# Seven block products in place of eight in both feed-forward layers of a two-block transformer chain, with the residual in DRAM meanwhile

## The chip, the cores and the metric

One core of a Trainium2 chip runs the whole chain in one launch. The metric is the device time of an execution in microseconds. Before the change the median of three runs is 2995.7 us (2993.17 to 2998.81). The engines are called as in the profile: PE multiplies matrices (PEld loads its weights beside it), DVE and ACT work on vectors, POOL is the general-purpose engine, SP issues transfers.

## The reference, cut to what matters

The first block (projections, an mLSTM branch, two attentions) is not touched. The second block has two layers; x is [1024 tokens, 1024 features], all float32:

```
h = modulate(rms_norm(x, norm1_g[0]), sh1, sc1);  x = x + g1 * s5_mixer(h)           # layer 0
h = modulate(rms_norm(x, norm2_g[0]), sh2, sc2);  x = x + g2 * swiglu(h)
h = modulate(rms_norm(x, norm1_g[1]), sh1, sc1);  x = x + g1 * short_conv_mixer(h)   # layer 1
h = modulate(rms_norm(x, norm2_g[1]), sh2, sc2);  x = x + g2 * swiglu(h)
return rms_norm(x, final_g)
def swiglu(h, w_in, w_out):      # w_in [1024, 2 * 2816], w_out [2816, 1024]
    g, u = jnp.split(h @ w_in, 2, axis=-1)
    return (jax.nn.silu(g) * u) @ w_out
```

The shifts, scales and gates of a layer come from one vector: mods = silu(c) @ w_ada[i] + b_ada[i].

## The kernel before, in words

**Operands.** Activations lie feature-major: a tile has 128 features on the partitions and 512 tokens (half of them) along a row; half 0 and half 1 are separate tiles. Every float32 operand of a product is an exact pair of parts, hi and lo: `Env.split` lets ACT copy the source to hi (L100) and DVE subtract to get lo (L108). `Env.mm3` (L110) then issues three matmuls, hi*hi, lo*hi, hi*lo (L114, L115, L116). So 128 x 128 weights against 512 tokens cost three matmuls, and `gemm` (L1629) runs eight such steps over the 1024 input features: 24 matmuls for 128 output features of 512 tokens.

**Feed-forward (`phase_ffn`, L1747).** The 2816 hidden features are 22 blocks f. `FGROUPS` (L31) puts them into groups of 5, 5, 4, 4, 4. For each f and each token half the kernel computes the gate (`pg`) and the value (`pu`), 48 matmuls, so 96 for one f; ACT takes silu of `pg` (L1765), DVE multiplies by `pu` (L1766), and the product is split into the pair `a`. The weights of one f come as two transfers of 512 KB and are split 128 x 1024 at a time. After a group the second product runs: 16 units `po` (eight output blocks, two token halves), each with three matmuls per f of the group, and DVE adds each result, times the gate, to the residual x, which stays in SBUF (L1788). In the last group the next norm is fed on the way: `Next.done` squares x on ACT and adds the squares on DVE (L220). In the second layer's last group token half 1 is cut in two parts of 256.

**Norms.** `Next.columns` sums the squares over the partitions on PE (`cs`, L159), DVE and POOL make 1/rms (L167, L170), DVE and PE spread it over the partitions (L193 to L200), and `Normed.pairs` (L1721) makes the pairs of the next product's input: a scalar_tensor_tensor on DVE (`hx`, L1739), a biased copy on ACT (L1742), a scalar_tensor_tensor on DVE (L1743). `Final` (L1839) is the last norm and the stores.

**The rest around it.** `phase_mixer` (L1639) ends with an output phase of 16 units of 48 matmuls. `phase_conv` (L1794) stands between the two feed-forward layers. `ada` (L1289) makes a layer's shifts and scales on DVE from 25 MB of weights, a step at each `e.tick()`; layer 1's run inside the first feed-forward layer, with tiles 512 wide. The pool of split weights, `e.wp`, lives on from phase to phase. Every engine works through its own queue in order; the order in the queues is set by a scheduler from the program order and not by hand here.

```
for f, h in seq:
    gemm(e, [ws[f][0]], hT, pg, h)
    gemm(e, [ws[f][1]], hT, pu, h)
    nc.scalar.activation(s, pg, AF.Silu)
    nc.vector.tensor_tensor(out=s, in0=pu, in1=s, op=ALU.mult)
    e.split(a[f][0][:, half(h)], a[f][1][:, half(h)], s)
```

Of the kernel before, what the change touches and what calls it, by code (L numbers as in the profile page):

```python
# [33 lines left out]
FGROUPS = [(0, 5), (5, 10), (10, 14), (14, 18), (18, 22)]  # L34


class Env:
    """Engines, pools, constants and DRAM operands shared by the phases."""
# [28 lines left out]

    def t2(self, name, dt=F32, w=HT):
# [16 lines left out]
    def psum(self, bufs):  # L85
        """A new set of PSUM pools: tag -> buffers."""
# [23 lines left out]
    def mm3(self, out, lhs, rhs, first, last):  # L110
        """out += lhs^T rhs, each operand an exact pair of parts."""
# [42 lines left out]
    def colsum(self, accs, name, tag="aux", n=4):  # L154
        """The sum of some [128, n * 128] -> PSUM columns [128 tokens, n] of sums over partitions."""
# [7 lines left out]
    def rstd(self, pc, pool, n, name, w=4):  # L163
        """(pc / n + eps) ** -0.5 of [128, w] columns."""
# [20 lines left out]
    def spread(self, r, pool, name, tag="aux", n=4):  # L185
        """The same by two products of exact parts, of n columns."""
# [51 lines left out]
# ---------------------------------------------------------------- block 1  # L238
def phase_projections(e):
    """Input norm, all input projections and the mLSTM branch."""  # L240
# [165 lines left out]
    def proj(m, name):  # L406
        """Feature-major projection block m: yields (half, PSUM)."""
# [20 lines left out]
    def proj_tok(evac):  # L428
        """Token-major projection to 256 columns; two token blocks a bank."""
# [17 lines left out]
    # z gates of the three branches, through DRAM, and the state-space tables  # L447
# [28 lines left out]
    # mLSTM: x_m, convolution, gates  # L476
# [20 lines left out]
    # mLSTM heads  # L497
# [13 lines left out]
    # on a row of both parts of a head's M: its negative, on every partition  # L511
# [8 lines left out]
    # gate weights folded through the q, k, v maps of each head  # L520
# [11 lines left out]
    for h in range(2):  # L532
        # the convolved and the plain inputs' parts side by side
# [45 lines left out]
    # decay of every (head, chunk) on all partitions  # L579
# [24 lines left out]
    def head(h4, prev):  # L604
# [9 lines left out]
        for h in range(2):  # L614
# [7 lines left out]
            # decay matrix, transposed: exp(a_s - M_t), s <= t  # L622
# [115 lines left out]
    # operands of the two attentions, through DRAM  # L738
# [18 lines left out]
def out_part(e, src, g, h, x, pair, done=None):  # L757
    """Adds branch g's part of the output projection to half h of x; yields between blocks."""
# [19 lines left out]
def phase_attention(e, r1, x, done):  # L778
    """Differential and memory attention, one half of the queries after the other; the output
    projection's parts that are ready fill the tensor engine. Gives y_d and y_c in DRAM."""  # L780
# [28 lines left out]
    # lambda on every partition  # L809
# [23 lines left out]
    class Diff:  # L833
        """One head and half of the differential attention; step j is queries j * 128 .. + 128."""
# [9 lines left out]
        def stages(self, j):  # L844
# [3 lines left out]
            def front():  # L848
                """Masked scores of both maps, their maxima and exponentials."""
# [5 lines left out]
                for c in range(nchunk):  # L855
# [3 lines left out]
                    for i, (a, b) in enumerate(((0, 0), (0, 1), (1, 0))):  # L859
                        # both maps side by side, each in its half of the rows  # L860
# [19 lines left out]
            def mid():  # L880
                """p0 - lam p1 l0 / l1, transposed."""
# [37 lines left out]
            def norm():  # L919
                """rmsnorm of od / l0, the gate."""  # L920
# [27 lines left out]
    class Mem:  # L948
        """One head and half of the memory attention; step i is queries i * 256 .. + 256."""
# [1103 lines left out]
```

## Time and profile before

| | |
|---|---|
| device time, median of 3 runs | 2995.7 us (2993.17 to 2998.81) |
| profiled execution: span (the page gives no other time of it) | 2994.1 us |
| PE busy | 2955.0 us, 14615 instructions |
| DVE busy | 1504.5 us, 2908 instructions |
| ACT busy | 950.5 us, 1692 instructions |
| POOL busy | 45.9 us, 62 instructions |
| mean DMA rate | 96 GB/s |
| mean granted PE clock | 0.990 of full speed |

The span runs from the first to the last instruction, and lies 1.6 us under the median of the runs. Busy times of PE add up records of pipelined matmuls that overlap, so the cost of a matmul is read from the distance of starts and not from the length of a record. The clock has two levels, 1.2 and 2.4 GHz; a figure between 0.5 and 1 is a mean over a stretch in which both were granted. The feed-forward layers begin at about 1172 and 2257 us; the convolution's products begin at 1904 us.

### The profile page before, as it was taken

The page shows a single profiled execution, that of the slowest core. Times are in us where ns is not written, and L with a number is a line of the kernel's source. Part 1 is how long each engine was busy: PE and PEld are TensorE (multiplying, and loading weights), DVE is VectorE, ACT ScalarE, POOL GpSimd, SP SyncE. Part 2 cuts the span into 40 slices and gives each one's busy share as a digit, 9 for nine tenths or more (in the row PEclk, how much of TensorE's full clock was granted, in tenths as well). Part 3 has the DMA queues.
Part 4 walks back from the last instruction along what each step waited for, and adds up shares of the span by engine and source line. Part 5 has one row for each costly group of instructions (what it writes and reads, how often), then busy time and mean ns, then how long its engine had stood idle before and what let it go on. Part 6 is the DMA issues. An engine that isn't in the chain of part 4 may idle for free.

```text
span 2994.1 us, 36875 instructions
## 1 busy us (share of the span) xinstructions
PE 2955.0 (99%) x14615; PEld 2419.5 (81%) x14615; DVE 1504.5 (50%) x2908; ACT 950.5 (32%) x1692; POOL 45.9 (2%) x62
## 2 busy tenths in 40 slices
PE   8999999999999999999999999999999999999999
PEld 7887788777777778888888888888888888888888
DVE  7988455588759845454443232722435232322324
ACT  6244652566646423211111112312323111111113
POOL 0000000000000000000000000000000000000000
PEclk9999999999999999999999999999999999999999
DMA  6465226643134621343331111111111111211111
GB/s 216 163 219 183 94 85 225 231 127 117 60 134 159 203 86 46 96 152 114 100 108 55 43 52 48 50 42 46 54 35 54 45 57 35 63 50 50 50 43 57
DMA packets 123334, 287.97 MB, mean 96 GB/s; under 512 B 12820, under 2 KB 30548, under 8 KB 122136
## 3 DMA queue, kind: packets, MB, share of 16 engines
q1 hardware_dynamic: 119576, 281.41, 29.5%
q10 hardware_dynamic: 3584, 4.20, 0.4%
q8 instruction: 115, 1.88, 0.3%
q14 instruction: 59, 0.48, 0.1%
HBM read 238.32 MB, written 47.24 MB: 95 GB/s over the span
## 4 chain that ended last, share of the span: by engine, by line
PE 83%; DVE 4%; issue 1%; DMA 1%; ACT 1%; POOL 0%; POOLq 0%; DVEq 0%; ACTq 0%; SPq 0%
PE po L114 5%; PE po L115 5%; PE po L116 5%; PE pu L115 5%; PE pu L114 5%; PE pu L116 5%; PE pg L114 5%; PE pg L115 5%; PE pg L116 5%; PE pout L114 1%; PE pout L115 1%; PE pout L116 1%; PE pS L863 1%; PE pgate L114 1%; PE pval L116 1%; PE pco L114 1%
## 5 line engine op out<-in xcount | busy, mean ns | idle before, releaser
L100 ACT ACTIVATE wh<-wraw 128x1024 fp32r<-128x1024 f32 (+2 forms) x285 | 270.0, 949 | 943.1 <-PE po L115 331.4
L108 DVE TENSOR_TENSOR wl<-wraw,wh 128x1024 fp32r<-128x1024 f32 (+2 forms) x285 | 308.4, 1083 | 293.4 <-ACT wh L100 290.8
L1766 DVE TENSOR_TENSOR silu<-pu,silu 128x512 f32<-128x512 f32 x88 | 60.8, 691 | 441.7 <-PE pu L116 441.7
L114 PE MATMUL po<-a,wh 128*128 128x512 f32 (+1 forms) x736 | 280.6, 381 | 0.0
L115 PE MATMUL po<-a,wh 128*128 128x512 f32 (+1 forms) x736 | 279.8, 380 | 0.0
L116 PE MATMUL po<-a,wl 128*128 128x512 f32 (+1 forms) x736 | 279.6, 380 | 0.0
L114 PE MATMUL pg<-f,wh 128*128 128x512 f32 x704 | 274.2, 389 | 0.0
L115 PE MATMUL pu<-f,wh 128*128 128x512 f32 x704 | 274.0, 389 | 0.0
L114 PE MATMUL pu<-f,wh 128*128 128x512 f32 x704 | 273.9, 389 | 0.0
L116 PE MATMUL pu<-f,wl 128*128 128x512 f32 x704 | 273.9, 389 | 0.0
L116 PE MATMUL pg<-f,wl 128*128 128x512 f32 x704 | 273.9, 389 | 0.0
L115 PE MATMUL pg<-f,wh 128*128 128x512 f32 x704 | 273.8, 389 | 0.0
L1788 DVE SCALAR_TENSOR_TENSOR x<-po,ada,x 128x512 f32<-128x512 f32 (+1 forms) x168 | 121.7, 725 | 203.3 <-PE po L116 203.2
L114 PEld LDWEIGHTS po<-a,wh 128*128 128x128 f32 x736 | 138.3, 188 | 30.1 <-ACT wh L100 3.2
L116 PEld LDWEIGHTS po<-a,wl 128*128 128x128 f32 x736 | 138.3, 188 | 26.3
L115 PEld LDWEIGHTS po<-a,wh 128*128 128x128 f32 x736 | 138.4, 188 | 26.0
L114 PEld LDWEIGHTS pg<-f,wh 128*128 128x128 f32 x704 | 132.0, 188 | 28.1 <-ACT wh L100 0.8
L114 PEld LDWEIGHTS pu<-f,wh 128*128 128x128 f32 x704 | 132.3, 188 | 27.5
L116 PEld LDWEIGHTS pg<-f,wl 128*128 128x128 f32 x704 | 132.3, 188 | 27.5
L115 PEld LDWEIGHTS pg<-f,wh 128*128 128x128 f32 x704 | 132.2, 188 | 27.4
L116 PEld LDWEIGHTS pu<-f,wl 128*128 128x128 f32 x704 | 132.0, 188 | 27.5
L115 PEld LDWEIGHTS pu<-f,wh 128*128 128x128 f32 x704 | 132.1, 188 | 27.3
(536 smaller groups left out, 5760.5 us busy)
## 6 DMA issues: line engine op xcount, KB each, us to landing
wraw<-in_w_ffn_in SPq DMA_DIRECT2D x88, 512.0 KB
wada<-in_w_ada SPq DMA_DIRECT2D x48, 512.0 KB
wada<-in_w_ada SPq DMA_DIRECT2D x96, 256.0 KB
wraw<-in_w_in SPq DMA_DIRECT2D x28, 512.0 KB
wraw<-in_w_out SPq DMA_DIRECT2D x48, 256.0 KB
wraw<-in_w_ffn_out SPq DMA_DIRECT2D x24, 512.0 KB
wraw<-in_conv_w_in SPq DMA_DIRECT2D x24, 512.0 KB
wraw<-in_w_ffn_out SPq DMA_DIRECT2D x32, 320.0 KB
```

The source lines that it names most:

```text
L100: i = self.nc.scalar.activation(*a, **k)
L108: nc.vector.tensor_tensor(out=lo, in0=src, in1=hi.bitcast(F32), op=ALU.subtract)
L114: nc.tensor.matmul(out, lh, rh, start=first, stop=False)
L115: nc.tensor.matmul(out, lh, rl, start=False, stop=False)
L116: nc.tensor.matmul(out, ll, rh, start=False, stop=last)
L863: nc.tensor.matmul(o[m], self.q[a][ms, qs], self.k[c][b][ms, 0:wc], start=(i == 0), stop=(i == 2 and not lastp))
L1766: nc.vector.tensor_tensor(out=s, in0=pu, in1=s, op=ALU.mult)
L1788: nc.vector.scalar_tensor_tensor(out=e.xt[m][:, tok], in0=pt, scalar=mod[:, 40 + m:41 + m], in1=e.xt[m][:, tok], op0=ALU.mult, op1=ALU.add)
```

## The change

Of one f the four results (gate and value, token half 0 and 1) are a 2 x 2 block matrix: rows gate and value, columns the token halves; the 1024 input features are the inner dimension, cut in two. The plain way takes eight products of half size, the new way seven (Strassen's method, in Winograd's form), each 12 matmuls: 84 for one f in place of 96.

- `Quad` replaces `Normed` before the feed-forward layers. It makes the norm's output in place in x's tiles, then forms the differences T1 to T4 of its blocks on DVE and splits seven kinds of block into pairs. Since x's tiles are used up by it, `Quad.done` first stores x to DRAM (`xd`) by 16 transfers of 256 KB from POOL's queue for each layer.
- `Weights` loads the weights of one f as four transfers of 256 KB, forms the sums S1 to S4 on DVE, and splits seven blocks of 128 x 512. Its pool is made anew for each feed-forward layer, and `e.wp` is released before it and made again for the convolution.
- `Unit` does the seven products of one f in the order 1 6 5 2 7 3 4 and combines them with seven additions on DVE, then as before silu, product and split.
- `ffn_head` does f = 0 in the plain way (96 matmuls) and f = 1 by seven products, interleaved, while `Quad`'s parts of the second token half are made.
- `FGROUPS` becomes 4, 4, 4, 4, 4, 2. In all groups but the last, ACT copies a unit of the second product out of PSUM times the gate (`ev`, three buffers), and a transfer from POOL's queue adds it to x in DRAM: 160 accumulating transfers of 256 KB in all. In the last group x is loaded back, and DVE adds to it as before.
- `ada` of layer 1 moves out of the feed-forward layer: its first half into the mixer's output phase, its second half into the convolution. The convolution copies four of x's blocks back into their first place (8 copies on ACT).

In the queues, PE has 10682 matmuls of 128 x 512 before and 10226 after, and 1538 of 128 x 256 before and 1442 after; DVE goes from 2814 instructions to 3483, SP from 815 to 985, POOL from 67 to 259.

```diff
-FGROUPS = [(0, 5), (5, 10), (10, 14), (14, 18), (18, 22)]
+FGROUPS = [(0, 4), (4, 8), (8, 12), (12, 16), (16, 20), (20, 22)]
...
+class Quad(Next):
...
+    def done(self, m, h):
+        super().done(m, h)
+        self.e.nc.gpsimd.dma_start(out=self.xd[m][:, half(h)], in_=self.x[m][h])
...
+    def make(self, h, r):
...
+        for k in range(4):
+            self.norm(h, k + 4, R)
+            self.parts2("11", k, x[k + 4][1])
+            if k % 2:
+                yield
+        for k in range(4):
+            self.norm(h, k, R)
+        for k in range(4):
+            tt(x[k + 4][1], x[k + 4][1], x[k][1], ALU.subtract)
+            tt(x[k][1], x[k][1], x[k][0], ALU.subtract)
+            self.parts2("T1", k, x[k][1])
+        yield
+        for k in range(4):
+            tt(x[k][0], x[k + 4][1], x[k][0], ALU.add)
+            self.parts2("T2", k, x[k][0])
+        for k in range(4):
+            self.parts2("T3", k, x[k + 4][1])
+        yield
+        for k in range(4):
+            tt(x[k + 4][0], x[k + 4][0], x[k][0], ALU.subtract)
+            self.parts2("T4", k, x[k + 4][0])
...
+            for o, a, b, op in (("S1", "10", "11", ALU.add), ("S2", "S1", "00", ALU.subtract),
+                                ("S3", "00", "10", ALU.subtract)):
+                nc.vector.tensor_tensor(out=st[o], in0=st[a], in1=st[b], op=op)
...
+class Unit:
+    order = "1652734"
+    left = dict(zip("1234567", ("00", "01", "S4", "11", "S1", "S2", "S3")))
+    right = dict(zip("1234567", ("00", "10", "11", "T4", "T1", "T2", "T3")))
...
+    def step(self, p):
...
+        product(e, b[p], self.W.take(), self.q, self.right[p], True, True)
...
+            e.nc.vector.tensor_tensor(out=t[o], in0=b["5" if o == "v" else p], in1=t[i], op=ALU.add)
...
-            gemm(e, [ws[f][0]], hT, pg, h)
-            inp.finish(NB)
-            gemm(e, [ws[f][1]], hT, pu, h)
...
+            ffn_head(e, W, inp, use(0), use(1))
+            fs = fs[2:]
+        for f in fs:
             e.tick()
+            Unit(e, W, q, use(f)).run(Unit.order)
...
+                t = e.ap.tile([P, HT], F32, tag="ev", name="ev", bufs=3)
+                nc.scalar.activation(t, pt, AF.Copy, scale=g)
+                nc.gpsimd.dma_start(out=inp.xd[m][:, tok], in_=t, accum_op=ALU.add)
...
+    u.run("65734")
```

**Order at the head of the first feed-forward layer, DVE.** The names: `f0v` is the variance behind the sums `cs` of token half 1, `f0R` the spread 1/rms, `f` the pairs of the norm's output, `raw` and `sum` weights as loaded and summed, `wl` their low parts, `ph` and `pu` results of products. Before, the rows behind that variance are:

```order
L167 TENSOR_SCALAR f0v<-cs 128x4
L1739 SCALAR_TENSOR_TENSOR hx<-x_5372,ada_4504,f0R 128x512
L1739 SCALAR_TENSOR_TENSOR hx<-x_5373,ada_4504,f0R 128x512
L1739 SCALAR_TENSOR_TENSOR hx<-x_5374,ada_4504,f0R 128x512
L1743 SCALAR_TENSOR_TENSOR f_11503<-hx,ada_4504,f_11502 128x512
```

After, some 60 rows behind the same variance (L172 there) stands a piece that has no counterpart before, with the sum S4 (L1868) and, three rows on, its low part:

```order
L2058 TENSOR_TENSOR p_11858<-ph_12059,p_11858 128x512
L2058 TENSOR_TENSOR p_11881<-ph_12086,p_11881 128x512
L113 TENSOR_TENSOR a_12056<-c_11999,a_12055 128x512
L1977 TENSOR_TENSOR p_11881<-p_11881,p_11858 128x512
L1868 TENSOR_TENSOR sum<-raw,sum 128x512
L1927 TENSOR_TENSOR uu<-pu_12115,p_11900 128x512
L113 TENSOR_TENSOR a_12056<-p_11881,a_12055 128x512
L113 TENSOR_TENSOR wl<-sum,wh 128x512
```

The last of these rows is the 76th instruction behind the variance, and product 3 of f = 1 on PE needs it.

**Order at the end of the first feed-forward layer, DVE and PE.** `po` are units of the second product, `c1sq` the sums of squares of token half 1, `cs` their sums over partitions, `pc`, `pv` and `pb` the convolution's first products. On DVE the last rows before the variance `cv` read, after the change:

```order
L2035 SCALAR_TENSOR_TENSOR x_16860<-po,ada_4504,x_16860 128x512
L225 TENSOR_TENSOR c1sq<-c1sq 128x512
L2035 SCALAR_TENSOR_TENSOR x_16861<-po,ada_4504,x_16861 128x512
L225 TENSOR_TENSOR c1sq<-c1sq 128x512
L2035 SCALAR_TENSOR_TENSOR x_16862<-po,ada_4504,x_16862 128x512
L225 TENSOR_TENSOR c1sq<-c1sq 128x512
L113 TENSOR_TENSOR wl<-wraw,wh 128x512
L172 TENSOR_SCALAR cv<-cs 128x4
```

They are as before but for the weight piece, 512 wide in place of 1024. PE's rows around that `cs` are, before:

```order
L114 MATMUL pb<-c_16126,wh 128x512
L115 MATMUL pb<-c_16127,wh 128x512
L159 MATMUL cs<-ones,c1sq 128x1 x8
L116 MATMUL pb<-c_16126,wl 128x512
L114 MATMUL pb<-c_16132,wh 128x512
```

and after:

```order
L119 MATMUL pv<-c_17007,wh 128x512
L120 MATMUL pv<-c_17008,wh 128x512
L119 MATMUL pb<-c_17007,wh 128x512
L120 MATMUL pb<-c_17008,wh 128x512
L164 MATMUL cs<-ones,c1sq 128x1 x8
L121 MATMUL pb<-c_17007,wl 128x512
L119 MATMUL pb<-c_17013,wh 128x512
```

Between the last `po` and the sums `cs` stood 24 of the convolution's matmuls, and now stand six.

## Rows read from the trace of the kernel before

**Rows 1.** The page's head: span; busy time, share and instructions of each engine.

```profile
span 2994.1 us, 36875 instructions
...
PE 2955.0 (99%) x14615; PEld 2419.5 (81%) x14615; DVE 1504.5 (50%) x2908; ACT 950.5 (32%) x1692; POOL 45.9 (2%) x62
```

**Rows 2.** PE's waits from 1000 us on: what for, total us, times, longest.

```profile
PE finR L199 <- DVE findh L193: 0.6, 1, 0.6
...
PE cs L159 <- ACT fin2sq L100: 0.2, 1, 0.2
```

**Rows 3.** Windows view: stretch, length, busy (count) by engine, PEclk, DMA share, GB/s.

```profile
990.00:1165.00 175.00, 175.00 (x773) 141.20 (x772) 93.41 (x119) 41.45 (x61) 1.01 (x1) 1.00 0.38 121
1290.00:1900.00 610.00, 609.42 (x2689) 499.51 (x2688) 235.38 (x311) 112.35 (x151) 1.01 (x1) 1.00 0.27 81
```

**Rows 4.** PE's timeline, end of the mixer: start, length (us); 31 starts apart.

```profile
1165.21 0.39 PE L115 MATMUL pgate<-yT,wh 128*128 128x512 f32 x1
...
1172.24 0.39 PE L116 MATMUL pval<-yT,wl 128*128 128x512 f32 x1
```

**Rows 5.** PE's timeline, last group of all: first unit, then 24 starts of 256.

```profile
2934.24 0.39 PE L114 MATMUL po<-a,wh 128*128 128x512 f32 x1
...
2936.96 0.28 PE L114 MATMUL po<-a,wh 128*128 128x256 f32 x1
...
2939.83 0.40 PE L114 MATMUL po<-a,wh 128*128 128x512 f32 x1
```

**Rows 6.** DVE's groups, 1290 to 1900 us: count, busy us, mean ns, idle.

```profile
L1788 DVE SCALAR_TENSOR_TENSOR x<-po,ada,x 128x512 f32<-128x512 f32 x76 | 56.9, 750 | 73.7 <-PE po L116 73.6
...
L1766 DVE TENSOR_TENSOR silu<-pu,silu 128x512 f32<-128x512 f32 x34 | 23.5, 691 | 162.0 <-PE pu L116 162.0
```

**Rows 7.** ACT's groups of the same stretch.

```profile
L100 ACT ACTIVATE a<-silu 128x512 fp32r<-128x512 f32 x34 | 21.5, 632 | 100.8 <-DVE silu L1766 100.8
```

**Rows 8.** DVE's timeline, start of the first feed-forward layer: start, length (us).

```profile
1172.73 0.75 DVE L1714 SCALAR_TENSOR_TENSOR sg<-pval,ada,sg 128x512 f32<-128x512 f32 x1 [3.42 <-PE pval L116]
1173.52 0.69 DVE L1716 TENSOR_TENSOR x<-x,sg 128x512 f32<-128x512 f32 x1
1174.13 1.22 DVE L108 TENSOR_TENSOR wl<-wraw,wh 128x1024 fp32r<-128x1024 f32 x1
1176.69 0.16 DVE L167 TENSOR_SCALAR f0v<-cs 128x4 f32<-128x4 f32 x1 [1.34 <-PE cs L159]
1176.77 2.06 DVE L1739 SCALAR_TENSOR_TENSOR hx<-x,ada,f0R 128x512 f32<-128x512 f32 x3
1178.74 2.07 DVE L1743 SCALAR_TENSOR_TENSOR f<-hx,ada,f 128x512 fp32r<-128x512 f32 x3
```

**Rows 9.** DVE's groups in the mixer's output phase, 1000 to 1172 us.

```profile
L1316 DVE SCALAR_TENSOR_TENSOR adacc<-wada,ada0c,adacc 128x1024 f32<-128x1024 f32 x20 | 25.7, 1284 | 14.4 <-DMA wada<-in_w_ada 14.3
```

**Rows 10.** Steps of the chain that ended last: start, length (us).

```profile
2960.84 1.53 PE cs L159 x14
...
2965.93 0.29 PE finR L200
...
2985.06 0.48 DVE x L1788
...
2988.27 0.75 DVE fin L1885
```

**Rows 11.** DVE's groups of 256 columns in the last 60 us.

```profile
L1788 DVE SCALAR_TENSOR_TENSOR x<-po,ada,x 128x256 f32<-128x256 f32 x16 | 7.7, 482 | 4.1 <-PE po L116 4.1
...
L220 DVE TENSOR_TENSOR fin2sq<-fin2sq 128x256 f32<-128x256 f32 x6 | 2.5, 423 | 1.4 <-ACT fin2sq L100 1.3
```

**Rows 12.** Windows view: a stretch of heavy transfers, two of many small products.

```profile
560.00:580.00 20.00, 20.00 (x103) 14.62 (x102) 17.09 (x47) 13.79 (x37) 0.00 (x0) 1.00 0.94 319
900.00:920.00 20.00, 18.81 (x149) 15.59 (x150) 18.35 (x20) 9.97 (x23) 1.31 (x6) 0.74 0.42 134
940.00:960.00 20.00, 18.32 (x191) 15.40 (x191) 19.86 (x26) 15.07 (x37) 3.30 (x6) 1.00 0.47 159
```

More of the change, by code (lines that the diff above doesn't have):

```diff
@@ L1366, in done @@
             self.finish()
-        self.sq[i].add(self.e.xt[m][:, self.parts[i]])
+        self.sq[i].add(self.e.xs(m, self.parts[i]))
         if m == NB - 1:
@@ new lines, in product, with __init__, run @@
+def product(e, out, w, q, c, first, last):
+    for k in range(4):
+        e.mm3(out, (w[0][:, k], w[1][:, k]), q[c, k], first and k == 0, last and k == 3)
+class Unit:
+    order = "1652734"
+    left = dict(zip("1234567", ("00", "01", "S4", "11", "S1", "S2", "S3")))
+    right = dict(zip("1234567", ("00", "10", "11", "T4", "T1", "T2", "T3")))
+    sums = {"6": [("u", "p")], "5": [("q", "u")], "2": [("p", "p")], "7": [("u", "u"), ("v", "u")],
+            "3": [("q", "q")], "4": [("u", "u")]}
+    done = {"2": "00", "7": "11", "3": "01", "4": "10"}
+    def __init__(self, e, W, q, use):
+        self.e, self.W, self.q, self.use, self.b, self.t = e, W, q, use, {}, {}
+    def run(self, ps):
+        for p in ps:
+            self.step(p)
+    def step(self, p):
+        e, t, b = self.e, self.t, self.b
+        b[p] = e.mm("mm", "pu" + p)
+        product(e, b[p], self.W.take(), self.q, self.right[p], True, True)
+        if p == "1":
+            t["p"] = e.t2("p1")
+            e.nc.scalar.activation(t["p"], b[p], AF.Copy)
+            return
+        for o, i in self.sums[p]:
+            if p == "2" and "u" not in t:
+                o = "c"
+            if o not in t:
+                t[o] = e.t2("u" + o)
+            e.nc.vector.tensor_tensor(out=t[o], in0=b["5" if o == "v" else p], in1=t[i], op=ALU.add)
+        if p in self.done:
+            self.use(self.done[p], t[o])
@@ L1744, in pairs, with phase_ffn, use, take @@
                                            op0=ALU.add, op1=ALU.subtract)
-def phase_ffn(e, L, mod, x, inp, nxt, mods=None):
-    nc, d, hT = e.nc, e.d, inp.hT
-    for gi, (f0, f1) in enumerate(FGROUPS):
-        a = {}
-        ws = {}
-        seq = [(f, h) for f in range(f0, f1) for h in range(2)]
+def phase_ffn(e, L, mod, inp, nxt, xp, last):
+    nc, d, q = e.nc, e.d, inp.q
+    W = Weights(e, 6, 6, 2, 3, 6)
+    e.ap = e.tc.alloc_tile_pool(name="ap", bufs=1, reuse_waits="tile")
+    src = lambda f: [d["w_ffn_in"][L, f + NF * i] for i in range(2)]
+    a = {}
+    def use(f):
+        s = {}
+        def take(n, t):
+            h = int(n[1])
+            s[h, int(n[0])] = t
+            if n[0] == "0":
+                nc.scalar.activation(t, t, AF.Silu)
+            if (h, 0) in s and (h, 1) in s:
+                nc.vector.tensor_tensor(out=s[h, 1], in0=s[h, 1], in1=s[h, 0], op=ALU.mult)
+                if f not in a:
+                    a[f] = tuple(xp.tile([P, T], F32R, tag="x", name=f"a{p}", bufs=NB) for p in range(2))
+                e.split(a[f][0][:, half(h)], a[f][1][:, half(h)], s[h, 1])
+        return take
+    std, u1 = W.unit(src(0), ("00", "10", "01", "11")), W.unit(src(1), [Unit.left[p] for p in "1265734"])
+    W.todo = [std[0], std[1], u1[0], std[2], std[3]] + u1[1:]
+    for gi, (f0, f1) in enumerate(FGROUPS):
+        for f in range(max(f0, 2), f1):
+            W.add(*W.unit(src(f), [Unit.left[p] for p in Unit.order]))
+        if f1 - f0 == 4:
+            W.add(*(W.block(d["w_ffn_out"][L, m, :, f0:f1]) for m in range(NB)))
+        else:
+            W.add(*(W.block(d["w_ffn_out"][L, m:m + 2, :, f0:f1].rearrange("m p f c -> p m f c"))
+                    for m in range(0, NB, 2)))
+    for gi, (f0, f1) in enumerate(FGROUPS):
+        end = gi == len(FGROUPS) - 1
+        fs = list(range(f0, f1))
@@ L1768, in phase_ffn @@
-        last = gi == len(FGROUPS) - 1
-        if last and mods:
-            e.drain()
-            nxt.mod = mods[1][0]
+            Unit(e, W, q, use(f)).run(Unit.order)
+        parts = nxt.parts if end else Next.parts
+        if end:
+            pool = last()
+            for m in range(4):
+                t = xp.tile([P, T], F32, tag="x", name=f"x{m}", bufs=NB)
+                nc.sync.dma_start(out=t, in_=inp.xd[m])
+                e.x[m] = [t[:, half(h)] for h in range(2)]
+            for m in range(4, NB):
+                t = pool.tile([P, T], F32, tag="x", name=f"x{m}", bufs=4)
+                e.x[m] = [t[:, half(h)] for h in range(2)]
+            for h in range(2):
+                for m in range(4, NB):
+                    nc.sync.dma_start(out=e.x[m][h], in_=inp.xd[m][:, half(h)])
@@ L1772, in phase_ffn @@
         wo = {}
-        nf = f1 - f0
-        nm = 8 // nf
-        parts = nxt.parts if last else Next.parts
-        for m, i in order(NB, NB - 1 if last else 0, len(parts)):
+        for m, i in (order(NB, NB - 1, len(parts)) if end else
+                     [(m, h) for m in (0, 1) for h in (1,)] + [(m, 0) for m in (0, 1)]
+                     + [(m, h) for m in range(2, NB) for h in range(2)]):
             tok = parts[i]
-            if m // nm not in wo:
-                g = m // nm * nm
-                wo[m // nm] = e.wload(d["w_ffn_out"][L, g:g + nm, :, f0:f1].rearrange("m p f c -> p m f c"),
-                                      (nm, nf, P))
-            e.tick()
+            if m not in wo:
+                w = W.take()
+                if f1 - f0 == 4:
+                    wo[m] = w
+                else:
+                    wo[m], wo[m + 1] = ([t[:, 2 * i:2 * i + 2] for t in w] for i in range(2))
@@ new lines, in phase_ffn, with ffn_head, mul, add @@
+    e.ap.release()
+    W.pool.release()
+def ffn_head(e, W, inp, use0, use1):
+    nc, q = e.nc, inp.q
+    u = Unit(e, W, q, use1)
+    t, w = {}, {}
+    def mul(name, k, c):
+        b = e.mm("mm", "ph" + name)
+        product(e, b, w[k], q, c, True, True)
+        return b
+    def add(o, b, i):
+        nc.vector.tensor_tensor(out=o, in0=b, in1=i, op=ALU.add)
+    inp.finish(2)
+    w["00"] = W.take()
+    for k in ("00", "10"):
+        if k not in w:
+            w[k] = W.take()
+        b = mul("a" + k, k, "00")
+        t[k] = e.t2("p" + k)
+        nc.scalar.activation(t[k], b, AF.Copy)
+    u.step("1")
+    inp.finish(2)
+    w["01"] = W.take()
+    c00 = e.t2("c00")
+    add(c00, mul("b00", "01", "10"), t["00"])
+    use0("00", c00)
+    w["11"] = W.take()
+    c10 = e.t2("c10")
+    add(c10, mul("b10", "11", "10"), t["10"])
+    u.step("2")
+    inp.finish(NB)
+    use0("10", c10)
+    for o, k in (("01", "00"), ("11", "10")):
+        b = e.mm("mm", "ph" + o)
+        product(e, b, w["01" if o == "01" else "11"], q, "11", True, False)
+        product(e, b, w[k], q, "T1", False, True)
+        add(t[k], b, t[k])
+        use0(o, t[k])
+    u.run("65734")
@@ L1827, in phase_conv @@
             e.split(yT[b][h][0], yT[b][h][1], yb[b, h])
+    e.drain()
+    for m in range(4, NB):
+        t = xp.tile([P, T], F32, tag="x", name=f"x{m}", bufs=NB)
+        for h in range(2):
+            nc.scalar.activation(t[:, half(h)], x[m][h], AF.Copy)
+        x[m] = [t[:, half(h)] for h in range(2)]
+    e.ap.release()
+    xq.release()
+    nxt.open()
     ws = {}
@@ L1836, in phase_conv @@
         nxt.done(m, h)
+    e.wp.release()
 class Final(Next):
```

212 lines of the change are left out of this document (156 added, 56 removed).

## The prediction, made before the changed kernel ran

> **What bounds the kernel now.** I read the page's head first: PE is busy for 99% of the span, DVE for half of it, ACT for a third [rows 1]. A busy PE may still be one that waits between short records, so I then read PE's waits from 1000 us on, where everything that the change touches lies: the longest is 0.6 us [rows 2]. The windows view of 1290 to 1900 us says the same of the first feed-forward layer: PE busy for 609.42 of 610 us at full clock, DVE for 235.38 [rows 3]. So the time there is the number of matmuls times their distance. That distance comes from the timeline: 31 starts of 128 x 512 in 7.03 us, 0.2268 us each, though a record is 0.39 long, since records overlap [rows 4]; and 24 starts of 128 x 256 in 2.87 us, 0.1196 each [rows 5]. Every matmul taken away gives its distance back, as long as DVE, ACT and the transfers keep pace.
>
> **What is removed.** The first product of 22 f in two layers takes 2 x 22 x 96 = 4224 matmuls before, and 2 x (96 + 21 x 84) = 3720 after: 504 x 0.2268 = 114.3 us less. The smaller last group moves second products from 256 to 512 columns: 48 more of 512 (+10.9) and 96 fewer of 256 (-11.5). PE's queue counts agree with both. Together **-114.9 us**.
>
> **A unit in the middle, f of 2 to 21: nothing.** PE needs 84 x 0.2268 = 19.05 us. DVE has 22 instructions of 512 columns: seven low parts of weights, four sums, seven additions, two products, two low parts of a. Two that follow each other start 0.61 us apart (1173.52 to 1174.13) [rows 8], which makes 13.4 us; at the full length of 0.69 [rows 6] 15.2. ACT has twelve of at most 0.63 [rows 7], 7.6. PE covers both; if it did not, every us over 19.05 would count some 40 times. The sums replace low parts of weights of 1024 columns, of 1.22 us each [rows 8], which are gone.
>
> **Second products: nothing.** A unit takes PE 12 x 0.2268 = 2.72 us. DVE's addition to x, 0.75 us [rows 6], goes; a copy on ACT, at most 0.63 [rows 7], and a transfer from POOL's queue come. With three buffers, copy and transfer hide while they take less than 3 x 2.72 = 8.16 us, so the transfer less than 7.5. Before has no accumulating transfer. The nearest row is the last store of 256 KB: its data are there at 2988.27 + 0.75 = 2989.02 and the span ends at 2994.1, 5.1 us [rows 1, 10]. As the addition reads and writes as much again, the ends are 5.1 and 10.2. I take 5.8: the bytes alone pass at 319 GB/s in 0.8 us [rows 12], and only they are doubled. The Trainium skill, page "SBUF — State Buffer", section "SBUF: two separate sides", speaks against this step: descriptors of a transfer that GpSimd issues cannot be written while a VectorE instruction holds the port the two share. No run here shows it; it would add one DVE instruction of up to 0.75 us [rows 6] to a transfer, 6.6 us, still hidden, so by the rule the sum stays, but there is less room.
>
> **Heads of both layers: DVE's queue sets the end.** In the first f the second token half's T1 to T4, all their pairs and the first weights pass through DVE in order. From the end of the last mixer product (1172.63) to the variance before takes 4.1 us [rows 4, 8]. Behind the variance the 76th instruction is the low part of S4, for which product 3 of f = 1 waits: 60 two-input instructions at 0.61, 8 scalar_tensor_tensor at 0.66 (three in 1.97) [rows 8] and 8 of 128 columns at about 0.25 (between the 0.16 of the variance and the 0.48 of 256 columns) [rows 8, 11], 43.9 us. It is ready 48.0 us after the last mixer product. Behind it PE still has 24 matmuls of f = 1 and 168 of f = 2 and 3, 43.5 us, so the group's products end at 91.5. Without a wait they would end after 348 x 0.2268 + 1.5 for the sums [rows 10] = 80.4. That is 11 us in each layer, **+22**. At full lengths instead of distances it is 16 each; at the better pace of the 1024-column piece (0.57 for 512) it is 8.
>
> **End of the first layer.** Its last group now has two f: a unit of 6 matmuls takes PE 1.36 us, and DVE one addition (0.66) and one sum of squares (0.61) for the same unit, with the norm of the first token half between them. From the last product on DVE has 32 scalar_tensor_tensor (21.1), 12 additions of squares (7.3) and one short `ada` step (0.5) until the sums of half 1 are complete; it starts after the first unit (1.8) and waits 5.4 us once for half 0's own sums, their 1/rms and its spread, as in the last group of all (2960.84 to 2966.22) [rows 10]. That is 36 us. PE has 104 matmuls before the same sums, with the sums of half 0 25 us, and then stands in its queue behind them. **+11 us**, with ends of 7 and 15. The convolution's 66 matmuls of half 0 behind it, 15 us, cover the norm that follows.
>
> **The last group of all.** Now 59.9 us from its first unit [rows 1, 5]. After, DVE paces it: 16 instructions of 512 for additions and stores (10.6), 6 sums of squares (3.7), 16 additions and 12 sums of squares of 256 at 0.40 and 0.34 (10.5; lengths of 0.48 and 0.42 less 0.085 as between length and distance at 512 [rows 8, 11]), small ones 2; waits for two norms of about 4 each [rows 8], 1.4 for the first unit and the 9.0 from the last addition to the end [rows 1, 10]. That is 45.2, or 14.7 less, where the matmul count has already booked 10.9 + 11.5 = 22.4 less: **+8**, ends 4 and 12.
>
> **The mixer's output phase.** It takes on 24 steps of `ada` of 1.28 us [rows 9], 31 us of DVE, where DVE has 93 of 175 us busy [rows 3]; 12.6 MB more raise 121 GB/s [rows 3] to 193, under the 319 reached elsewhere [rows 12]. PE covers it. For SP's queue, now past more waits there and at the reloads of x, I add **2** (0 to 10).
>
> **The clock.** After a pause the lower level may be granted. At 900 us a stretch with PE busy for 18.81 of 20 us has a mean of 0.74; at 940 us one with 18.32 keeps 1.00 [rows 12]. What runs slowly while DVE sets the pace costs nothing. At 0.74 all matmuls behind the three waits (192, 192, 66) would cost 36 us; I take **4**.
>
> **Sum.** -114.9 + 22 + 11 + 8 + 2 + 4 = -68 us, against the profiled span of 2994.1, which lies 1.6 us under the median of 2995.7: **2928 us**. A measurement can tell some 0.2%, 6 us, from no change.
>
> **Rivals.**
> - *The waits are covered* (12%): DVE runs ahead at head and border, because the scheduler moved the low parts early. For it: the better pace of the 1024-column piece; against it: the queue order itself. 2995.7 - 114.9 + 8 = 2889.
> - *The accumulating transfers bound the second products* (7%, slower). Beyond 7.5 us each further us costs a third per unit of 160. The 68 us are gone at 7.5 + 3 x 68/160 = 8.8 us. At the upper end of 10.2 it is 2.7 x 160/3 = 144 more, 3072. For it: read, add and write in place of one write; against it: the doubling of bytes alone is under 1 us. The skill's rule on the shared port would push this way.
> - *The clock stays low behind the waits* (14%): 32 us more than booked, 2960.
> - *DVE's queue holds up every unit* (9%): additions stand in order behind low parts that wait on ACT, and PE waits 1 us in each of 40 units, 2968. Against it: 19.05 to 13.4.
> - That fewer products are not issued is excluded by the counts in the queues.
>
> **Numbers.** The forecast has 58%. Its own ends reach from about 2910 to 2945. Taking in the clock, the held-up units and the near half of the covered case, the range is 2893 to 2966. Faster by over 0.2%: all but the transfers' case and a worse one among the held-up units, 0.92; within 0.2%: 0.01; slower: 0.07.
>
> **What would show it.** PE about 115 us less; distances of matmuls still 0.2268; PE waits of some 10 us each at both heads for `wl` from `sum`, and at the end of the first layer for `cs` behind DVE's squares; no wait of ACT for `ev` buffers. PE idle inside units, or ACT waiting for a POOL transfer, would make it wrong.

## The result and the profile after

The changed kernel takes 2963.1 us (median of 4 runs, 2956.0 to 2965.2) against 2995.3 before: a ratio of 0.989, 95% interval 0.9875 to 0.9903, or 32 us less. The forecast was 68 less, 2928; its range, 2893 to 2966, holds the measured time near its upper end. Half of the expected gain is missing, and one term of the sum has most of it. That the range holds the time is luck: its upper end stood for a clock that stays low behind the waits (2960) and for units held up by DVE (2968), and neither is the main cause.

The page of the changed kernel, its head, the chain by engine and the accumulating transfers (KB each, median us from issue to landing):

```profile
span 2961.8 us, 38430 instructions
...
PE 2865.6 (97%) x14064; PEld 2336.5 (79%) x14064; DVE 1831.7 (62%) x3577; ACT 1223.2 (41%) x2259; POOL 198.5 (7%) x254
...
PE 75%; DVE 7%; DMA 4%; issue 1%; ACT 1%; POOL 0%; DVEq 0%; POOLq 0%; SPq 0%; ACTq 0%
...
f0x<-ev POOLq DMA_DIRECT2D x80, 256.0 KB, 4.3
```

Against [rows 1], PE has 551 fewer instructions and 89 us less of busy time, but stands idle for 96 us of the span where it did for 39. Transfers have gone from 1% in the page of before to 4% of the chain, and by the chain's own lines 3 of the 4 are `wada` loads, the weights of `ada`. PE's waits from 990 us on (us in total, times, longest), which answer to [rows 2]:

```profile
PE pada L1330 <- DVE adacc L1321: 22.7, 6, 11.7
PE pc L119 <- ACT wh L105: 5.5, 1, 5.5
PE pu L119 <- ACT wh L105: 5.0, 3, 2.9
PE cs L164 <- DVE c1sq L225: 5.0, 1, 5.0
PE pfin L2188 <- DVE x L2035: 3.7, 1, 3.7
PE cs L164 <- ACT f01sq L105: 2.6, 1, 2.6
```

The lower five belong to the heads, the border and the end, places that the forecast had priced. The first is `ada`'s sum over partitions in the mixer's output phase, a place to which the forecast gave 2 us.

Stages, from the first and last matmuls of `pgate`, `pval`, `pc` and `pco` in the two traces, in us:

| stage | before | after | difference | forecast |
|---|---|---|---|---|
| mixer's output phase (first pgate to last pval) | 182.3 | 215.8 | +33.5 | +2 |
| first feed-forward layer (to the first pc) | 731.9 | 683.9 | -48.0 | -57 + 11 |
| border and convolution (to the last pco) | 352.6 | 366.8 | +14.2 | +11 |
| second feed-forward layer and end | 737.4 | 704.2 | -33.2 | -58 + 11 + 8 |

(The forecast for a layer is 21 x 12 x 0.2268 = 57 us, the clock's 4 us not assigned.) The last three rows together are 67 us less, where the forecast had 74 less, or 70 with the clock's 4; the first row alone takes back half of that. Of its 33.5 us, some 3 are the three moved sums themselves (1.08 us each), which the first feed-forward layer no longer has.

### The profile page after: what moved, and what is told of

It is laid out like the page before. It is cut to its first block, busy times and chain, and to the rows that moved or that the text cites. A ratio compares the mean times of both kernels' runs of the same rounds, so it can differ in the third digit from the quotient of the medians.

```text
span 2961.8 us, 38430 instructions
## 1 busy us (share of the span) xinstructions
PE 2865.6 (97%) x14064; PEld 2336.5 (79%) x14064; DVE 1831.7 (62%) x3577; ACT 1223.2 (41%) x2259; POOL 198.5 (7%) x254
## 4 chain that ended last, share of the span: by engine, by line
PE 75%; DVE 7%; DMA 4%; issue 1%; ACT 1%; POOL 0%; DVEq 0%; POOLq 0%; SPq 0%; ACTq 0%
PE pu L119 9%; PE pu L120 9%; PE pu L121 9%; PE po L119 6%; PE po L120 6%; PE po L121 6%; DMA wada<-in_w_ada 3%; PE pout L119 1%; PE pS L868 1%; PE pout L120 1%; PE pout L121 1%; PE pb L121 1%; PE pc L119 1%; PE pc L121 1%; PE pv L121 1%
## 5 line engine op out<-in xcount | busy, mean ns | idle before, releaser
L105 ACT ACTIVATE wh<-raw 128x512 fp32r<-128x512 f32 x264 | 165.2, 630 | 376.5 <-PE pu L120 201.7
L113 DVE TENSOR_TENSOR wl<-raw,wh 128x512 fp32r<-128x512 f32 x264 | 180.7, 686 | 205.2 <-ACT wh L105 204.4
L119 PE MATMUL pu<-f,wh 128*128 128x512 f32 x672 | 262.6, 391 | 3.0 <-ACT wh L105 2.9
L120 PE MATMUL pu<-f,wh 128*128 128x512 f32 x672 | 262.2, 390 | 0.0
L105 ACT ACTIVATE wh<-wraw 128x512 fp32r<-128x512 f32 (+1 forms) x189 | 136.0, 726 | 253.6 <-PE pj L120 40.0
L113 DVE TENSOR_TENSOR wl<-wraw,wh 128x512 fp32r<-128x512 f32 (+1 forms) x189 | 152.1, 808 | 117.7 <-ACT wh L105 113.0
L113 DVE TENSOR_TENSOR wl<-sum,wh 128x512 fp32r<-128x512 f32 x126 | 85.9, 685 | 135.3 <-ACT wh L105 135.3
L2039 ACT ACTIVATE ev<-po,ada 128x512 f32<-128x512 f32 x160 | 108.6, 679 | 123.1 <-issue 62.1
L105 ACT ACTIVATE wh<-sum 128x512 fp32r<-128x512 f32 x126 | 78.6, 628 | 179.0 <-PE pu L120 108.7
L119 PE MATMUL pj<-h,wh 128*128 128x512 f32 x352 | 140.3, 399 | 0.0
L120 PE MATMUL pj<-h,wh 128*128 128x512 f32 x352 | 139.5, 396 | 0.0
L121 PE MATMUL pj<-h,wl 128*128 128x512 f32 x352 | 139.2, 395 | 0.0
```

The costliest lines, as they stand in the source:

```text
L113: nc.vector.tensor_tensor(out=lo, in0=src, in1=hi.bitcast(F32), op=ALU.subtract)
L119: nc.tensor.matmul(out, lh, rh, start=first, stop=False)
L120: nc.tensor.matmul(out, lh, rl, start=False, stop=False)
L121: nc.tensor.matmul(out, ll, rh, start=False, stop=last)
L2039: nc.scalar.activation(t, pt, AF.Copy, scale=g)
```

## Where the time went: the mixer's output phase

DVE's timeline in the changed kernel, around the third sum (start us, length us, idle before and its releaser):

```profile
1052.40 1.28 DVE L1321 SCALAR_TENSOR_TENSOR adacc<-wada,ada0c,adacc 128x1024 f32<-128x1024 f32 x1 [0.85 <-DMA wada<-in_w_ada]
...
1058.16 1.28 DVE L1321 SCALAR_TENSOR_TENSOR adacc<-wada,ada0c,adacc 128x1024 f32<-128x1024 f32 x1 [0.64 <-DMA wada<-in_w_ada]
...
1061.95 1.28 DVE L1321 SCALAR_TENSOR_TENSOR adacc<-wada,ada0c,adacc 128x1024 f32<-128x1024 f32 x1 [1.90 <-DMA wada<-in_w_ada]
1064.51 1.28 DVE L1321 SCALAR_TENSOR_TENSOR adacc<-wada,ada0c,adacc 128x1024 f32<-128x1024 f32 x1 [1.27 <-DMA wada<-in_w_ada]
```

and PE's, at the same sum and its neighbours:

```profile
1042.03 1.08 PE L1330 MATMUL pada<-adacc,ones 128*64 128x512 f32 x4 [1.69 <-DVE adacc L1321]
...
1065.94 1.97 PE L1330 MATMUL pada<-adacc,ones 128*64 128x512 f32 x4 [11.71 <-DVE adacc L1321]
...
1099.01 1.11 PE L1330 MATMUL pada<-adacc,ones 128*64 128x512 f32 x4 [2.82 <-DVE adacc L1321]
```

A step of `ada` takes 1.28 us on DVE, but the steps come some 3 us apart, because most of them wait for their load of 512 KB. Eight steps make a sum, so a sum can be had every 24 us (1042.03 to 1065.94). In PE's queue, only 48 matmuls, 11 us, lie between the second sum and the third; PE goes through its queue in order, and stands at the sum until the loads have come.

The distance comes from an edit that neither the description of the change nor the forecast names. A sum takes three calls of `e.tick()`: four loads and their steps, the other four, then the matmuls `pada`. Before, each of the 16 units called it once; the change, with twice the work to place, calls it twice:

```diff
-        e.tick()
...
+        for _ in range(2):
+            e.tick()
```

So a sum stood three units, 144 matmuls, behind the one before, and now stands two units or one. Before:

```profile
1035.40 1.08 PE L1325 MATMUL pada<-adacc,ones 128*64 128x512 f32 x4
...
1069.28 1.08 PE L1325 MATMUL pada<-adacc,ones 128*64 128x512 f32 x4
```

They came 33.9 us apart, and PE never waited. Yet the loads were no faster then. DVE's last step of the second and of the third sum before:

```profile
1037.18 1.28 DVE L1316 SCALAR_TENSOR_TENSOR adacc<-wada,ada0c,adacc 128x1024 f32<-128x1024 f32 x1
...
1062.79 1.29 DVE L1316 SCALAR_TENSOR_TENSOR adacc<-wada,ada0c,adacc 128x1024 f32<-128x1024 f32 x1 [0.18 <-DMA wada<-in_w_ada]
```

The two lie 25.6 us apart, and the second sum was complete at 1038.46, 31 us before PE asked for it at 1069.28.

**Theories.** A: PE stands in its queue at `pada`, because the sums are now asked for faster than the loads can come; A1, that two buffers set the pace of the loads, A2, that the rate of the transfers does, A3, that it is the amount that was moved in. B: the phase got longer through the mixer's own weights, now in 256 KB blocks, or through the stores of x. C: the missing time is in the feed-forward layers after all.

### Most of the moved work left out

```diff
...
-    e.bg += [ada(e, wada, 0, mods, 4, 1, 1, 3), ada(e, wada, 1, mods, 4, 1, 1, 0, 3)]
+    e.bg += [ada(e, wada, 0, mods, 4, 1, 1, 3), ada(e, wada, 1, mods, 4, 1, 1, 0, 3, ks=1)]
```

(`ks` is the number of loads in a sum; the lines of `ada` that take it are left out here.)

> Leaves out seven of eight loads and sums of the first three parts of layer 1's shifts and scales in the mixer's output phase; all else is the changed kernel. Theory A (PE stands in its queue before the sums pada until ada's loads have come, 22.7 us in six waits, and loses the clock around them): the phase goes back from 209 to about 177 us, in all 2963 - 32 = 2931. Rival B (the phase is long because the mixer's own weights now come as 256 KB blocks and x is stored from POOL's queue, whatever ada does): no change, 2960 to 2965. Rival C (the missing 35 us of the forecast were lost in the feed-forward layers' heads and at the border): 2955 or more.

Measured: 2949.8 us (2947.8 to 2953.4), between A's 2931 and B's 2960, so both figures missed. PE still waits at `pada`:

```profile
PE pada L1332 <- DVE adacc L1323: 12.9, 2, 10.3
```

The work that was moved in is nearly all gone here, and yet more than half of the wait is left. It stands at the sums of layer 0, which were in this phase before: those are asked for at twice the pace too. So theory A has the place right, but I had the wrong steps in mind; B and C, which left the time where it was or near it, cannot explain the 13 us that came back. This made the pace itself worth a run.

### The moved work alone, in the kernel before

```diff
-    e.bg.append(ada(e, lambda n: rp.tile([P, T], F32, tag=n, name=n, bufs=2), 0, mods, 4, 1, 1, 3))
+    wada = lambda n: rp.tile([P, T], F32, tag=n, name=n, bufs=2)
+    e.bg += [ada(e, wada, 0, mods, 4, 1, 1, 3), ada(e, wada, 1, mods, 4, 1, 1, 0, 3)]
...
-        e.tick()
+        for _ in range(2):
+            e.tick()
...
```

> The kernel before, with one part of the change alone: layer 1's first three parts of shifts and scales in the mixer's output phase, with two steps for each unit, and only the last three in the first feed-forward layer. Theory A: the whole price shows without any seven-product code, 2995 + 25 to 35 = 3020 to 3030. Rivals B and C: 2995, no change.

Measured: 3027.0 us (3024.1 to 3028.4) against 2993.5 for the kernel before, run beside it, ratio 1.0112, interval 1.0096 to 1.0127: 33.5 us slower. That is the whole price, without any of the seven-product code, and B and C are out: in the trace the phase takes 216.6 us, where the changed kernel has 215.8. Its wait in the trace:

```profile
PE pada L1325 <- DVE adacc L1316: 20.4, 5, 8.7
```

### The pace alone, in the kernel before

```diff
-        e.tick()
+        for _ in range(2):
+            e.tick()
```

> The kernel before with a single edit: two steps of ada for each unit of the mixer's output phase in place of one; no more loads, nothing else of the change. Theory A1 (the pace: the three sums pada now stand 97 and 49 matmuls apart in PE's queue, 22 and 11 us, where 145 matmuls or 33 us were, and eight loads through two buffers take 23): PE waits 10 to 15 us there, 3005 to 3015. Rival A3 (the amount: 12.6 MB more of transfers and 31 us more of DVE made the price): no change, 2992 to 2997.

Measured: 3009.8 us (3008.1 to 3010.9) against 2993.7, ratio 1.0056, interval 1.0041 to 1.0071. Not one byte more is loaded, and the kernel is 16 us slower. So A3 is not the whole cause: the pace alone makes half of the 33.5 us, and the other half comes only when three more sums are asked for at that pace. The trace:

```profile
PE pada L1325 <- DVE adacc L1316: 14.2, 2, 10.7
```

### Four buffers for the loads

```diff
-    wada = lambda n: rq.tile([P, T], F32, tag=n, name=n, bufs=2)
-    e.bg += [ada(e, wada, 0, mods, 4, 1, 1, 3), ada(e, wada, 1, mods, 4, 1, 1, 0, 3)]
+    wada = lambda n: rq.tile([P, T], F32, tag=n, name=n, bufs=4 if n == "wada" else 2)
+    e.bg += [ada(e, wada, 0, mods, 4, 1, 3, 3), ada(e, wada, 1, mods, 4, 1, 3, 0, 3)]
```

> The changed kernel with four buffers for ada's weights in place of two in the mixer's output phase, three loads ahead. Theory A1 (each load waits for its buffer, about 2.9 us a step, so two buffers set the pace): PE's waits for pada fall from 23 to under 8 us, 2940 to 2950. Theory A2 (the transfers' rate of about 240 GB/s sets the pace): waits stay at 15 us or more, 2955 to 2963. Rivals B and C: 2963.

Measured: 2932.3 us (2930.8 to 2934.8), ratio to before 0.9797, interval 0.9783 to 0.9812. That is 31 us less than the changed kernel, with every moved byte still loaded, and better than any of the expectations. The wait at `pada` is 0.5 us. What changed is the pace of the loads, as the windows view tells (stretch, length, busy time by engine, PEclk, DMA share, GB/s). The changed kernel:

```profile
1002.00:1102.00 100.00, 82.81 (x345) 63.05 (x344) 65.82 (x79) 20.98 (x36) 3.49 (x6) 0.94 0.67 210
```

and with four buffers:

```profile
1010.00:1110.00 100.00, 99.44 (x430) 76.55 (x429) 84.70 (x104) 27.17 (x47) 5.11 (x9) 1.00 0.79 270
```

The transfers reach 270 GB/s over 100 us in place of 210, so their rate was no limit, and A2 falls. The groups of DVE show it from the other side. Changed kernel, 1000 to 1207 us:

```profile
L1321 DVE SCALAR_TENSOR_TENSOR adacc<-wada,ada1c,adacc 128x1024 f32<-128x1024 f32 x21 | 27.0, 1284 | 21.6 <-DMA wada<-in_w_ada 21.6
L1321 DVE SCALAR_TENSOR_TENSOR adacc<-wada,ada0c,adacc 128x1024 f32<-128x1024 f32 x20 | 25.7, 1284 | 17.3 <-DMA wada<-in_w_ada 17.3
```

With four buffers, 995 to 1176 us:

```profile
L1321 DVE SCALAR_TENSOR_TENSOR adacc<-wada,ada0c,adacc 128x1024 f32<-128x1024 f32 x21 | 26.9, 1279 | 4.0 <-DMA wada<-in_w_ada 3.8
L1321 DVE SCALAR_TENSOR_TENSOR adacc<-wada,ada1c,adacc 128x1024 f32<-128x1024 f32 x21 | 26.8, 1278 | 2.9 <-DMA wada<-in_w_ada 2.7
```

The steps are as long as before; only the idle time ahead of them is gone, 39 us of it down to 7.

### The sums evenly spread, with four buffers and with two

```diff
-    e.bg += [ada(e, wada, 0, mods, 4, 1, 1, 3), ada(e, wada, 1, mods, 4, 1, 1, 0, 3)]
+    e.bg += [ada(e, wada, 0, mods, 2, 1, 1, 3), ada(e, wada, 1, mods, 2, 1, 1, 0, 3)]
...
-        for _ in range(2):
+        for _ in range(3 if (2 * m + h) % 4 == 0 else 2):
```

With four buffers, three loads ahead:

> As with four buffers, and ada's steps spread evenly over the output phase (steps of two loads; three ticks in one unit, two in the next three), so that the sums pada stand about 97 matmuls or 22 us apart in PE's queue in place of 49 to 97. Theory A1: waits nearly gone, 2931 to 2936. Theory A2: eight loads take about 24 us against 22, so some 2 us at each sum, 2940 to 2950. Rivals B and C: 2963.

Measured: 2931.4 us (2928.7 to 2932.4), the same as with four buffers alone.

With the two buffers of the changed kernel:

> The changed kernel with its two buffers, but ada's steps spread evenly, so that the six sums stand some 97 matmuls or 22 us apart. Theory A1: eight loads at 2.9 us want 23 us, so 1 to 2 us of wait at each sum and little loss of clock, 2938 to 2948. Rival A4 (two buffers are too few whatever the spacing): 2955 or more.

Measured: 2936.6 us (2931.7 to 2937.1), a little under the expected range; one wait at `pada` of 3.3 us is left. So two buffers are enough, but for some 4 us, when the sums stand 23 us or more apart, and bunched sums are no harm when the loads come fast. A1 holds in this form: the price is the sum's distance in PE's queue against the time of eight loads.

## The other terms, tried on top of four buffers

### Two buffers for the accumulating transfers

```diff
-                t = e.ap.tile([P, HT], F32, tag="ev", name="ev", bufs=3)
+                t = e.ap.tile([P, HT], F32, tag="ev", name="ev", bufs=2)
```

> The changed kernel with four buffers for ada, and two buffers in place of three for the copies that the accumulating transfers read. A unit takes PE 2.72 us, so a buffer may be held for 5.44. If copy (0.67) and landing (4.3) are all that holds it, 5.0 us: no change against 2932. If the issue on POOL (0.85) comes on top, 5.8 us: up to 0.18 us in each of 160 units, 2935 to 2962. Three buffers allow 8.16 and hide either.

Measured: 2932.9 us (2932.0 to 2933.3) against 2932.3 with three. The second products have room to spare, and nothing here bears out the slower rival of the forecast. But the transfers do not always fit into 5.44 us: with two buffers ACT now stands for transfers that have not landed (us in total, times, longest),

```profile
ACT ev L2039 <- DMA f0x<-ev: 46.0, 33, 3.7
ACT ev L2039 <- DMA f1x<-ev: 39.2, 33, 2.2
```

85 us in all, where with three buffers no such wait is seen. PE does not stand for it: it is busy for 500.00 of 500 us from 1300 on in this run too. So the wait costs nothing, as ACT has slack here.

### A last group of four f

```diff
-FGROUPS = [(0, 4), (4, 8), (8, 12), (12, 16), (16, 20), (20, 22)]
+FGROUPS = [(0, 4), (4, 6), (6, 10), (10, 14), (14, 18), (18, 22)]
...
-        for m, i in (order(NB, NB - 1, len(parts)) if end else
+        for m, i in (order(NB, 4, len(parts)) if end else
```

(The tiles of the reloaded x and of the convolution change places to make room.)

> The changed kernel with four buffers for ada, and a group of two f second in place of last: groups of 4, 2, 4, 4, 4, 4, so that a unit of the last group takes PE 2.72 us in place of 1.36; all of x is reloaded into the pool that was for half of it, and the last four output blocks, not the last seven, go half by half. Against the run with four buffers alone (2932). Theory D (short units, in which DVE sets the pace, make the loss at the border to the convolution and at the end): the border gives back 8 to 12 us and the end 4 to 8, less 0 to 5 for short units in the middle, 2912 to 2922. Rival E (the border's loss is the convolution's weights, late behind x's reload in SP's queue): PE's wait for wh at pc stays at 5 us or grows, 2925 to 2935.

Measured: 2920.5 us (2919.4 to 2923.6), ratio to before 0.9759, interval 0.9743 to 0.9776, 12 us less than with four buffers alone, within D's range. From first `pc` to last `pco` the stage falls from 367.3 to 360.8 us, which is 6.5 where D had 8 to 12, and the second layer with the end from 701.9 to 697.6, the 4.3 being at the low end of D's 4 to 8. The border in the changed kernel, on PE's timeline:

```profile
1890.77 0.79 PE L119 MATMUL pc<-c,wh 128*128 128x512 f32 x1 [5.55 <-ACT wh L105]
...
1898.87 3.55 PE L164 MATMUL cs<-ones,c1sq 128*128 128x1 f32 x16 [4.98 <-DVE c1sq L225]
...
1902.85 0.63 PE L119 MATMUL pb<-c,wh 128*128 128x512 f32 x1
1903.27 0.63 PE L120 MATMUL pb<-c,wh 128*128 128x512 f32 x1
```

and in this run:

```profile
1861.14 0.79 PE L119 MATMUL pc<-c,wh 128*128 128x512 f32 x1 [5.09 <-ACT wh L105]
...
1862.11 0.56 PE L164 MATMUL cs<-ones,c1sq 128*128 128x1 f32 x2 [0.17 <-DVE c1sq L225]
```

The wait for DVE's squares is gone, as D has it; the wait for the convolution's weights stays, as E has it. The matmuls behind the pause start 0.42 us apart, nearly twice the 0.2268 of [rows 4]: the granted clock from 1902 to 1905 us is 0.50, the lower level, a second price of a pause.

### The convolution's weights first in SP's queue

```diff
...
+                if keep:
+                    e.tc.keep_in_program_order(i0)
...
-        e.tick()
+        if (b, h) != (0, 0):
+            e.tick()
```

> On top of the run with the group of two f second: the convolution's first six weight loads stand ahead of ada's loads in SP's queue (ada's first step one unit later, its loads kept in program order). Against 2920.5 of that run. Theory F (ada's loads, hoisted to the border, wait for their two buffers and hold SP's queue in front of the convolution's weights): PE's wait of 5.1 us for wh at pc falls under 2 and the slow clock behind it gets shorter, 2912 to 2917. Rival G (the weights' tiles themselves come free only with the last units' operands): the wait stays, 2918 to 2922.

Measured: 2920.2 us (2918.7 to 2923.6), no change, and the wait at `pc` is still 4.6 us. F falls. ACT's timeline in this run shows what the weights' copies stand behind:

```profile
1852.03 1.38 ACT L1955 ACTIVATE c<-hx,ada 128x512 fp32r<-128x512 f32 x2 [0.69 <-DVE hx L1952]
1855.34 0.63 ACT L105 ACTIVATE c1sq<-x 128x512 f32<-128x512 f32 x1 [1.93 <-DVE x L2032]
1855.93 1.38 ACT L1955 ACTIVATE c<-hx,ada 128x512 fp32r<-128x512 f32 x2
1857.22 2.17 ACT L105 ACTIVATE wh<-wraw 128x512 fp32r<-128x512 f32 x4
```

The weights need no wait of their own there: their four copies stand in ACT's queue behind the norm's, which wait for DVE. That G is the other reason, memory that comes free late, isn't shown by this; the run only shows that SP's queue is not it.

### More work for DVE in the heads

```diff
+        more = e.t2("more")
+        for k in range(8):
+            tt(more, x[k % 4 + 4][1], x[k % 4][1], ALU.subtract)
```

> On top of the run with the group of two f second: eight more subtractions of 128 x 512 on DVE (their result is not used) in each head, between the pairs of T3 and those of T4. Against 2920.5 of that run. Theory D2 (DVE's queue sets the end of both heads, as the forecast has it): each head longer by 8 x 0.61 = 4.9 us, 2928 to 2932. Rival H (ACT's copies or the weights set it, DVE has room): 2919 to 2924.

Measured: 2933.7 us (2932.4 to 2935.6), 13 us more than 2920.5 and a little above D2's 2932. The head of the first layer, from the last `pval` to the first `po`, goes from 93.8 to 98.4 us, 4.6 more, and that of the second, from the last `pco`, from 93.9 to 99.0, 5.1 more, both near the 4.9 of eight instructions. The mixer's end already lies 2.8 us later in this profiled execution, ahead of the added instructions. DVE's queue sets the heads, and H falls.

## Why the prediction was wrong, step by step

- **The mixer's output phase: the step that failed.** The forecast said that PE covers it, for 0 to 10 us, as DVE is busy for 124 of 175 us and the transfers rise to 193 GB/s. Both figures are means over the phase. What decides is a chain that no mean shows: PE's queue has a sum, the sum needs eight steps in order on DVE, each step needs a load, each load one of two buffers. The measured price is 33.5 us. And the forecast counted how many steps were moved in, not how often PE would now ask for a sum. [rows 9] had the sign: of 14.4 us in which DVE was idle before `ada`'s steps, 14.3 were put down to `wada` loads. The queue's order had the other half, 144 matmuls between sums before and 96, 48 and then 85 or more after. 48 x 0.2268 = 11 us against eight steps of 2.9 or 3 gives a wait of 12 to 13 at the third sum; it measured 11.71. The forecast read the 1.28 us of a step from [rows 9] and left the rest of the row aside.
- **Matmuls removed: right.** PE is busy for 500.00 of 500 us in the middle of the first layer and for 400.00 of 400 in the second:

```profile
1300.00:1800.00 500.00, 500.00 (x2207) 414.02 (x2206) 256.33 (x395) 183.44 (x301) 60.55 (x71) 1.00 0.45 90
2400.00:2800.00 400.00, 400.00 (x1766) 331.20 (x1766) 216.77 (x334) 147.21 (x241) 40.90 (x48) 1.00 0.42 86
```

  DVE at 51% and 54% there never holds up a unit, and the rival of held-up units falls with it. But PE's busy time fell by 89 us, not by the 115 that the forecast gave as a sign. That fits a clock granted at 0.979 on the mean, where it was 0.990, which lengthens the matmuls that are left.
- **Second products: right, with room.** The accumulating transfers land after 4.3 us (median; 3.6 to 5.9), where 5.8 was taken and 7.5 allowed. The rule of the Trainium skill that was weighed there, on the page "SBUF — State Buffer", section "SBUF: two separate sides", would lengthen them while a VectorE instruction holds the shared port. The trace does not tell which instructions hold it, so it neither bears the rule out nor refutes it; with DVE busy for half of the time the slowest took 5.9, so no delay that matters is to be seen.
- **Heads: size right, in part by luck, place not quite.** The first group's products were to end 91.5 us after the mixer's last and end at 92.1 in the first layer (1207.4 to 1299.5) and at 94.2 in the second. DVE's queue sets them, as the run with more work for it shows. But PE waited at product 6, whose S2 copy and low part come late, and not at product 3; and only 6.5 of the 11.7 us over the unhindered 80.4 are waits, 2.6 of them at the norm's sums. The rest goes with the clock, whose mean granted level is 0.96 from 1207 to 1300 us; the forecast had counted all 11 as one wait. PE's timeline at product 6:

```profile
1243.65 0.50 PE L119 MATMUL pu<-T2f,wh 128*128 128x512 f32 x1 [1.99 <-ACT wh L105]
...
1245.99 0.50 PE L121 MATMUL pu<-T2f,wl 128*128 128x512 f32 x1 [1.61 <-DVE wl L113]
```

- **Border: 14 against 11.** The wait at the squares came as described, 5.0 us; the weights' copies behind the norm on ACT, 5.5 us, were not in the forecast, and the slow clock behind both waits only as a part of the clock's 4 us.
- **The last group: 49.3 us against 45.2** (2912.55, its first unit, to 2961.8). DVE paces it only in part: PE's 7.0 us of waits there all name DVE, but `po` matmuls on PE are 41% of the chain over these 50 us.
- **The clock: under-sized where it mattered.** The forecast booked 4 us, for the heads and the border alone. There, by an estimate from how far beyond 0.2268 us the matmuls start apart, waits not counted, it is 4.6 and 6.0 us in the two heads and 4.6 at the border and in the convolution. In the mixer's phase four buffers gave back 28 of their 31 us (215.8 to 187.5): 22.2 are PE's waits (22.7 to 0.5), and most of the other 6 go with the slow level around them; the mean granted clock of the phase rises from 0.95 to 1.00. The 3 us outside the phase stay open. Two windows of the changed kernel:

```profile
1058.00:1078.00 20.00, 12.06 (x45) 8.44 (x46) 8.09 (x11) 4.00 (x8) 0.89 (x2) 0.74 0.51 164
1118.00:1138.00 20.00, 18.41 (x81) 14.22 (x80) 13.41 (x16) 5.26 (x9) 1.08 (x2) 1.00 0.80 240
```

The pause of 11.7 us lies in the first of these, with a mean of 0.74; the second has a pause of 1.6 us and keeps 1.00.

With the buffers mended the time is 2932, where the forecast was 2928. By the stages of the table above, that run has the mixer's phase 5 us longer than before (2 forecast; 3 are the moved sums), the first layer 47 shorter (46), border and convolution 15 longer (11) and the second layer with the end 35 shorter (39), with 4 more booked for the clock.

## What to carry to other kernels

Background work that is moved takes its own pace along: before it is called covered, follow its chain to the first in-order queue that waits for it, and set the distance of those waits in that queue against the time of the loads behind them, with the number of buffers that there are. Idle time put down to a transfer, on an engine that is not the bound, is that chain's warning and costs nothing only as long as the consumer is asked late enough. And where units get shorter, ask at once which other engine serves each of them: in this kernel a group of two f last, at the border and at the end, cost 12 us more than the same group in second place.

## What the runs showed of the hardware that was not expected

An accumulating transfer of 256 KB into DRAM landed in 4.3 us (median of 160, 3.6 at least). The plain stores of the same size from the same queue landed in 3.0 us (median) before the first layer and in 2.3 before the second, 2.3 at least:

```profile
f0x<-x POOLq DMA_DIRECT2D x16, 256.0 KB, 3.0
...
f1x<-x POOLq DMA_DIRECT2D x16, 256.0 KB, 2.3
```

So the accumulating kind took 1 to 2 us longer; they ran at different places, so how much of that is the addition stays open. Its issue holds POOL for 0.85 us, against 0.54 for the plain one. In the mixer's output phase all transfers together reached 210 GB/s over 100 us while the loads of 512 KB had two buffers, and 270 GB/s when they had four.
